# A hybrid encoder block on one core: the delta rule's stream moved to the front of the scan, and the order of the y blocks in the output projection

## The chip, the core and the metric

The kernel runs on one core of a Trainium2 chip. The time is device microseconds of one execution. The engines: PE (TensorE, with its weight load PEld), DVE (VectorE), ACT (ScalarE), POOL (GpSimd) and SP (SyncE, which issues most of the transfers). Each engine takes its instructions strictly in the order of its queue.

## What is computed

One encoder block on x of 512 tokens by 2048 features, in fp32. After a norm and one input projection, 16 heads of 128 go through two recurrences, 8 heads each, each scanned in both directions and summed; then a norm by head with a gate, one output projection, a residual sum, and a SwiGLU feed-forward.

```python
# group A, gated delta rule, per chunk of 64 (fwd and bwd summed)
w = u_c - einsum("bhrk,bhkv->bhrv", wk_c, S0)
o = einsum("bhrk,bhkv->bhrv", qd_c, S0) + einsum("bhrj,bhjv->bhrv", a_c, w)
S1 = gl_c * S0 + einsum("bhjk,bhjv->bhkv", kd_c, w)
# group B, HGRN2, per chunk of 32 (fwd and bwd summed)
A = sum(q_c * k_c * dec); o = (q_c * exp(Bc)) @ S0 + A @ v_c
S1 = exp(Bc[-1]) * S0 + (k_c * exp(Bc[-1] - Bc)).T @ v_c
# then: y = gated norm of both groups by head; x + y @ w_out; SwiGLU block
```

The recurrences of different heads don't depend on one another. The output projection sums over all heads of both groups.

## The kernel before

**Stages.** Projections of the input up to about 849 us of the span, then the scan, the output projection, gate and up, and down. The big products are split in high and low parts (oh, ol for the operands; whr, whs, wlr, wls for the weights) and done by seven products of half blocks.

**The scan** (`scan`, L836) runs two kinds of streams beside one another, each in pairs of heads 0, 2, 4, 6.

The delta rule is called gdn. `gdn_blocks` (L537) inverts the blocks of a pair: it loads tile L, sets P0 and P1 to zero (POOL, L549), loads into them, and goes through small matmuls L569/570, L578/579, L593/594 and L600/601 with transposes L586/587 on DVE. `gdn_pair` (L607) then does the recurrence of the pair: loads kq2 (L613, L614), vt, qd (L625); kt on DVE (L624); qd and L are multiplied on POOL (L626, L627). There are four steps. In a step: ks on PE (L645, not in the first step), rr on DVE (L649), matmul by P (L653), copy to w on ACT (L656), state on PE (L660) and S on DVE (L668 in the first step, L665 after), and the output oT on PE (L632). kq2, kt and qd have one buffer each; L has one for each of two pools, which the pairs take in turn. The blocks of the next pair run beside the recurrence of a pair.

HGRN2 is called hgrn (`hgrn_pair`, L678): loads hf, hq, hv (L686 to L688), four arrays X (ACT, DVE L694, POOL L695) and kc (POOL L697), then levels of 1, 2, 4, 8 and 16 and of 32 and 64: a copy kc on ACT (L719), matmuls (L722, L738), a predicated copy to C on DVE (L725), four updates of X on DVE (two of L748 and two of L750), and a product tot on POOL (L753) that the next level's updates need. At the end come transposes and their copies hkt, three steps with L781 and the state hS (L785, L788), and the output oT by L771 and L794. X of pairs 0 and 4 lies in one pool, X of pairs 2 and 6 in another, with one buffer each.

Each pair of either kind ends with `finish` (L437): squares, a sum by a matmul with ones (L445), ln and exp on ACT, two products on DVE (L448 and, with the gate gt loaded at L450, L451) and the store to d_y (L452).

**What sets the order.** The two kinds and the pairs are Python generators that yield a modelled time behind each part. `merge` (L815) takes the next part always from the stream whose modelled time is least; the first named wins a tie. A pair of numbers and streams like (40, a, b) is one stream that begins at 40 of modelled time and runs a, then b. A scheduler that simulates the engines' time lines then orders the instructions within what the code's order and the dependencies allow. Before, hgrn pairs 0 and 4 begin at 0, hgrn pairs 2 and 6 at 40, and gdn at 40, with hgrn's parts counted at 0.75 of their modelled time.

**The output projection** (`out_proj`, L870) first loads y back in blocks of two heads' pairs (tile yt, L892), in the order `Y_BLOCKS`: entry 0 is heads 0 to 3 of gdn, 2 its heads 4 to 7, 4 heads 0 to 3 of hgrn, 6 its heads 4 to 7. `operands` (L945) makes tsum (DVE, L941 to L943), oh (ACT, L956) and ol (DVE, L958) from each. `block_weights` (L962) loads the weights (raw, L972), sums them on DVE (L974 to L976), and splits them (L980 to L986). `step` issues the big matmuls (L1022) in the same order of blocks. The first tile yt lies, before and after, in memory that X of hgrn pairs 2 and 6 used, so its load waits until these are done.

Of the kernel before, what the change touches and what calls it, by code (L numbers as in the profile page):

```python
# [70 lines left out]
class Block:  # L71
# [769 lines left out]
    def scan(self):  # L841
        tc = self.tc
        with ExitStack() as st:
            pool = lambda name, **k: st.enter_context(tc.tile_pool(name=name, reuse_waits="tile", **{"bufs": 1, "side": "right", **k}))
            for n, b in (("psh", 2), ("pss", 2), ("poh", 1), ("pog", 1)):
                setattr(self, n, st.enter_context(tc.tile_pool(name=n, bufs=b, space=PSUM, reuse_waits="tile")))
            first, second, rest = pool("sca"), pool("scb"), pool("scc")
            self.sca = Pools(rest, hf=first, hq=first, C=first, X=second)
            self.sch, self.fin = pool("sch"), pool("fin")
            self.scb = pool("sc1"), pool("sc2", side="left")  # L850
            self.sc = pool("sc")
            self.gdn_ready = {}

            def gdn():
                yield from self.gdn_blocks(0)
                for i in range(0, H, 2):
                    yield from self.merge((0, self.gdn_pair(i)), *([(0, self.gdn_blocks(i + 2))] if i + 2 < H else []))

            def faster(i):
                for dt in self.hgrn_pair(i):  # L860
                    yield 0.75 * dt

            for _ in self.merge((0, faster(0), faster(4)), (40, faster(2), faster(6)), (40, gdn())):
                pass


    Y_BLOCKS = (0, 4, 6, 2)
    Y_SLOTS = (6, 7, 0, 1, 2, 3, 4, 5)

    def out_proj(self, late):  # L870
# [17 lines left out]
        yops = [None] * (KT // 2)  # L888
        for q, j in enumerate(self.Y_BLOCKS):
            for b in range(2):  # L890
# [3 lines left out]
        for ps in ((0, 1), *((p,) for p in range(2, KT // 2))):  # L894
            prods = self.block_products([(a["w_out"][0], 2 * p * P) for p in ps], 0, yops, order=self.Y_BLOCKS)
            for p, prod in zip(ps, prods):
# [292 lines left out]
```

## Time and profile before

| | us |
|---|---|
| median of 3 runs | 2677.78 (2677.45 to 2679.18) |
| the profiled execution | 2677.02 |
| its span | 2675.2 |
| PE busy | 2489.8 (93% of the span) |
| DVE busy | 2298.1 (86%) |
| ACT busy | 1497.4 (56%) |
| POOL busy | 519.9 (19%) |
| mean granted PE clock | 0.968 of full |

PE is the fullest engine over the whole span. The 40 slices of the page (66.9 us each) show where it isn't: in slices 13 to 17, about 803 to 1137 us, PE is 60 to 90% busy, and the granted clock is down to 0.8 there. That is the scan and the beginning of the output projection, and the views in the rows below are of that part. A busy share there is an average over places with different limits.

### The profile page before, as it was taken

To read this page: it belongs to the slowest core of one execution; us is meant where nothing else is said; L and a number is where in the kernel's file an instruction comes from. 1 tells how busy PE (TensorE), PEld (TensorE's weight loads), DVE (VectorE), ACT (ScalarE), POOL (GpSimd) and SP (SyncE) were. 2 spreads that over 40 slices of the span, in tenths; PEclk is the share of its full clock that TensorE was granted. 3 is DMA by queue.
4 is the path that set the end of the run, shared out by engine and by line. 5 is a ranking of instruction groups with operands and counts; after the bars stand their busy time and mean duration, and the time that the engine had idled before them with its cause. 6 is when DMAs were issued, how large, how long until landed. Compare 5 with 4: busy or idle time off the path is not lost.

```text
span 2675.2 us, 55501 instructions
## 1 busy us (share of the span) xinstructions
PE 2489.8 (93%) x22511; PEld 2437.7 (91%) x22511; DVE 2298.1 (86%) x3598; ACT 1497.4 (56%) x2057; POOL 519.9 (19%) x400
## 2 busy tenths in 40 slices
PE   7999999989997788799999999999999989998996
PEld 6999999889986667799899999999999989998996
DVE  7989989998976876877988989889889888888885
ACT  7787777666665433656644444444444455655664
POOL 1233224443333532222000000000000012222221
PEclk9999999999998888999999999999999999999998
DMA  8889999999897443799343344333333388887875
GB/s 228 191 200 210 212 204 223 232 220 239 200 233 201 108 122 113 220 243 251 118 135 127 123 123 126 122 116 121 125 114 123 121 250 196 213 190 178 195 157 142
DMA packets 401708, 465.71 MB, mean 174 GB/s; under 512 B 48449, under 2 KB 354043, under 8 KB 401451
## 3 DMA queue, kind: packets, MB, share of 16 engines
q1 hardware_dynamic: 310939, 311.67, 38.3%
q0 software_dynamic: 71936, 103.83, 24.2%
q10 hardware_dynamic: 18576, 46.67, 5.0%
q8 instruction: 176, 2.88, 0.4%
q14 instruction: 81, 0.66, 0.1%
HBM read 303.66 MB, written 54.62 MB: 134 GB/s over the span
## 4 chain that ended last, share of the span: by engine, by line
PE 67%; DMA 10%; DVE 9%; issue 7%; ACT 4%; POOL 1%; SPq 1%; ACTq 0%; DVEq 0%; POOLq 0%
PE big L1022 64%; DMA wlr<-raw 4%; DMA raw<-in_w_out 1%; DVE X L750 1%; DVE wls L986 1%; DVE X L748 1%; DMA acc<-d_rows 1%; DMA tt<-d_t 1%; DMA raw<-in_w_down 1%; ACT wlr L980 1%; ACT whs L985 0%; ACT whr L981 0%; DVE wsum L975 0%; DMA sl<-d_l 0%; DVE wsum L974 0%
## 5 line engine op out<-in xcount | busy, mean ns | idle before, releaser
L985 ACT CAST whs<-wsum 128x1024 fp32r<-128x1024 f32 (+1 forms) x448 | 461.8, 1033 | 470.2 <-PE big L1022 242.4
L986 DVE TENSOR_TENSOR wls<-wsum,whs 128x1024 fp32r<-128x1024 f32 (+1 forms) x448 | 563.2, 1258 | 151.4 <-ACT whs L985 146.7
L982 POOL DMA_DIRECT2D wlr<-raw x272 | 323.7, 1190 | 1889.1 <-DVE tsum L941 893.8
L1022 PE MATMUL big<-oh,whs 128*128 128x256 f32 x2368 | 661.8, 283 | 3.7 <-ACT whs L985 3.7
L1022 PE MATMUL big<-ol,whs 128*128 128x256 f32 x2368 | 661.4, 282 | 0.0
L1022 PE MATMUL big<-oh,wls 128*128 128x256 f32 x2368 | 646.4, 283 | 3.3 <-DVE wls L986 3.3
L1022 PE MATMUL big<-oh,wlr 128*128 128x256 f32 x1776 | 493.4, 282 | 23.0 <-DMA wlr<-raw 22.8
L1022 PE MATMUL big<-oh,whr 128*128 128x256 f32 x1776 | 499.4, 283 | 13.2 <-ACT oh L956 9.8
L1022 PE MATMUL big<-ol,whr 128*128 128x256 f32 x1776 | 496.7, 281 | 0.6 <-DVE ol L958 0.6
L1022 PEld LDWEIGHTS big<-oh,whs 128*128 128x128 f32 x2368 | 449.9, 190 | 5.0 <-ACT whs L985 5.0
L1022 PEld LDWEIGHTS big<-ol,whs 128*128 128x128 f32 x2368 | 450.4, 190 | 0.0
L1022 PEld LDWEIGHTS big<-oh,wls 128*128 128x128 f32 x2368 | 443.3, 191 | 4.4 <-DVE wls L986 3.9
L1022 PEld LDWEIGHTS big<-oh,wlr 128*128 128x128 f32 x1776 | 332.9, 189 | 26.8 <-DMA wlr<-raw 26.5
L1022 PEld LDWEIGHTS big<-oh,whr 128*128 128x128 f32 x1776 | 335.7, 189 | 17.5 <-ACT oh L956 12.6
L974 DVE TENSOR_TENSOR wsum<-raw 128x512 f32<-128x512 f32 (+1 forms) x448 | 314.5, 703 | 42.0 <-DMA raw<-in_w_out 20.2
L1022 PEld LDWEIGHTS big<-ol,whr 128*128 128x128 f32 x1776 | 335.2, 189 | 1.9 <-DVE ol L958 1.7
L1022 PE MATMUL big<-tp,whs 128*128 128x256 f32 x1728 | 322.8, 283 | 2.7 <-ACT whs L985 2.7
L981 ACT CAST whr<-raw 128x768 fp32r<-128x768 f32 (+1 forms) x272 | 221.6, 815 | 157.2 <-PE big L1022 155.9
L1022 PEld LDWEIGHTS big<-tp,whs 128*128 128x128 f32 x1728 | 270.0, 192 | 3.9 <-ACT whs L985 3.1
L1022 PE MATMUL big<-tp,wls 128*128 128x256 f32 x864 | 242.7, 286 | 24.4 <-DVE wls L986 24.4
L980 ACT ACTIVATE wlr<-raw 128x768 fp32r<-128x768 f32 (+1 forms) x272 | 224.4, 825 | 58.9 <-DMA raw<-in_w_out 23.6
L985 ACT CAST whr<-raw 128x768 fp32r<-128x768 f32 x176 | 146.8, 835 | 159.0 <-PE big L1022 156.8
(319 smaller groups left out, 4699.4 us busy)
## 6 DMA issues: line engine op xcount, KB each, us to landing
wlr<-raw POOLq DMA_DIRECT2D x256, 384.0 KB, 5.9
raw<-in_w_in SPq DMA_DIRECT2D x144, 512.0 KB, 4.9
raw<-in_w_gate SPq DMA_DIRECT2D x88, 512.0 KB, 3.6
raw<-in_w_up SPq DMA_DIRECT2D x88, 512.0 KB, 3.6
raw<-in_w_down SPq DMA_DIRECT2D x80, 512.0 KB, 4.6
raw<-in_w_out SPq DMA_DIRECT2D x32, 512.0 KB, 5.9
d_t<-yt ACTq DMA_DIRECT2D x22, 512.0 KB, 2.9
tt<-d_t ACTq DMA_DIRECT2D x22, 512.0 KB, 4.5
```

The costliest lines, as they stand in the source:

```text
L748: nc.vector.tensor_tensor(out=xv[:, 0:2, n, 0, :], in0=xv[:, 0:2, n, 0, :], in1=tv[:, :, n, 1:2].broadcast_to([P, 2, nb // 2, hs]), op=ALU ...
L750: nc.vector.tensor_tensor(out=xv[:, 2:4, n, 1, :], in0=xv[:, 2:4, n, 1, :], in1=tv[:, :, n, 0:1].broadcast_to([P, 2, nb // 2, hs]), op=ALU ...
L974: tt(out=sm[:, :, 0:2], in0=raw[:, :, 0:1].broadcast_to([P, n, 2, P]), in1=raw[:, :, 1:3], op=ALU.add)
L980: nc.scalar.mul(out=lo, in_=src_, mul=-1.0)
L981: nc.scalar.copy(out=hi, in_=src_)
L982: nc.gpsimd.dma_start(out=lo.rearrange("p j x n -> p j (x n)").bitcast(F32), in_=src_.rearrange("p j x n -> p j (x n)"), accum_op=ALU.add)
L985: nc.scalar.copy(out=hi, in_=src_)
L986: tt(out=lo, in0=src_, in1=hi.bitcast(F32), op=ALU.subtract)
L1022: mm = lambda a, b, s, e: nc.tensor.matmul(prod[i], lhsT=a, rhs=b, start=s, stop=e, skip_group_check=True)
```

## The change

The scan's `merge` gets its streams in another order: gdn is named first and begins at 0, with its parts counted at 0.8 of their modelled time; hgrn 0 and 4 begin at 0 as before, hgrn 2 and 6 at 40 as before. `paced` is the former `faster` with the factor as an argument. And the output projection takes the blocks of y in the order gdn 0 to 3, hgrn 0 to 3, gdn 4 to 7, hgrn 4 to 7, where hgrn 4 to 7 came ahead of gdn 4 to 7 before. No instruction of the computation is added or left out. Behind the change, the line numbers of the kernel after are larger by one.

```diff
-            def faster(i):
-                for dt in self.hgrn_pair(i):
-                    yield 0.75 * dt
-
-            for _ in self.merge((0, faster(0), faster(4)), (40, faster(2), faster(6)), (40, gdn())):
+            def paced(steps, x):
+                for dt in steps:
+                    yield x * dt
+
+            hgrn = lambda i: paced(self.hgrn_pair(i), 0.75)
+            for _ in self.merge((0, paced(gdn(), 0.8)), (0, hgrn(0), hgrn(4)), (40, hgrn(2), hgrn(6))):
                 pass
 
-    Y_BLOCKS = (0, 4, 6, 2)
+    Y_BLOCKS = (0, 4, 2, 6)
```

**DVE, gdn pair 2.** In the queue of DVE before, around the second and third rr of the pair (X_11312 belongs to hgrn 4, sh_11984 to the finish of another pair):

```order
L649 SCALAR_TENSOR_TENSOR rr_11933<-sc_11928,ngam_1220,vt_11626 128x128 x4
L748 TENSOR_TENSOR X_11312<-X_11312,tot16_11926 128x2x8x32
L750 TENSOR_TENSOR X_11312<-X_11312,tot16_11926 128x2x8x32
L748 TENSOR_TENSOR X_11312<-X_11312,tot16_11926 128x2x8x32
L750 TENSOR_TENSOR X_11312<-X_11312,tot16_11926 128x2x8x32
L448 SCALAR_TENSOR_TENSOR sh_11984<-oT_11616,cols_307,sh_11984 128x1024
L451 TENSOR_TENSOR sh_11984<-sh_11984,gt_11993 128x1024
L665 SCALAR_TENSOR_TENSOR S_11950<-S_11722,glast_1222,sc_11945 128x128 x4
L649 SCALAR_TENSOR_TENSOR rr_12002<-sc_11997,ngam_1220,vt_11626 128x128 x4
```

The same place of DVE after, from the pair's first S to the first S of pair 4 (kt_11703 and S_11795 are pair 4's, X_10971 is of hgrn 2):

```order
L668 COPY S_11136<-sc_11131 128x512
L586 STREAM_TRANSPOSE q64_11068<-P0_11070 32x32 x8
L587 STREAM_TRANSPOSE q64_11068<-P1_11079 32x32 x8
L649 SCALAR_TENSOR_TENSOR rr_11285<-sc_11280,ngam_1220,vt_11040 128x128 x4
L665 SCALAR_TENSOR_TENSOR S_11302<-S_11136,glast_1222,sc_11297 128x128 x4
L649 SCALAR_TENSOR_TENSOR rr_11391<-sc_11386,ngam_1220,vt_11040 128x128 x4
L665 SCALAR_TENSOR_TENSOR S_11408<-S_11302,glast_1222,sc_11403 128x128 x4
L649 SCALAR_TENSOR_TENSOR rr_11437<-sc_11432,ngam_1220,vt_11040 128x128 x4
L624 TENSOR_TENSOR kt_11703<-sc_11705,kdc_1221 128x1024
L624 TENSOR_TENSOR kt_11703<-sc_11714,kdc_1221 128x1024
L448 SCALAR_TENSOR_TENSOR sh_11516<-oT_11064,cols_307,sh_11516 128x1024
L451 TENSOR_TENSOR sh_11516<-sh_11516,gt_11525 128x1024
L668 COPY S_11795<-sc_11790 128x512
L748 TENSOR_TENSOR X_10971<-X_10971,tot8_11584 128x2x16x16
```

Before, updates of X stand between the rr of a pair; after, none stands between the three rr of pair 2, and the next update of X is queued behind the first S of pair 4.

**PE, the end of the scan.** Before, from the last L794 on (oT_12891 is the output of hgrn 6, the rows of L622, L653, L660, L632 and L645 are gdn 6's; the first big matmul of the output projection stands 16 rows below the first row here):

```order
L794 MATMUL oT_12891<-X_12107,hS_13005 128x128 x4
L622 MATMUL sc_12918<-ident_61,kq2_12911 128x128 x4
L622 MATMUL sc_12927<-ident_61,kq2_12911 128x128 x4
L653 MATMUL sc_12937<-vt_12912,P0_12394 128x128
L653 MATMUL sc_12937<-vt_12912,P1_12403 128x128
L653 MATMUL sc_12937<-vt_12912,P0_12394 128x128
L653 MATMUL sc_12937<-vt_12912,P1_12403 128x128
L445 MATMUL sc_13056<-sq_13053,ones_69 128x512
L445 MATMUL sc_13059<-sq_13053,ones_69 128x512
L660 MATMUL sc_12944<-w_12942,kt_12916 128x128 x4
```

PE after, from the last L794 of hgrn 6 on:

```order
L794 MATMUL oT_13045<-X_12504,hS_13066 128x128 x4
L794 MATMUL oT_13045<-X_12504,hS_13080 128x128 x4
L445 MATMUL sc_13096<-sq_13093,ones_69 128x512
L445 MATMUL sc_13099<-sq_13093,ones_69 128x512
L1023 MATMUL big_13274<-oh6_13164,whr_13284 128x256
L1023 MATMUL big_13277<-oh6_13164,whr_13284 128x256
L1023 MATMUL big_13275<-oh6_13164,whr_13284 128x256
```

Before, the whole recurrence of gdn 6 stands behind hgrn 6's last output; after, it stands ahead of it, and the output projection follows hgrn 6's finish.

**POOL, around gdn pair 2.** After, the two-input products that stand in one row on POOL beside the stretch of DVE above (L626 of gdn 2, L627 of gdn 4, L695 and L697 of hgrn 4):

```order
L753 TENSOR_TENSOR tot1_11956<-hf_11649 128x2x512
L626 TENSOR_TENSOR qd_11045<-qd_11045,kq2_11039 128x1024 x2
L753 TENSOR_TENSOR tot2_12113<-tot1_11956 128x2x256
L753 TENSOR_TENSOR tot64_12016<-tot32_11842 128x2x8
L695 TENSOR_TENSOR X_11655<-hq_11648,hf_11649 128x1024
L753 TENSOR_TENSOR tot4_12205<-tot2_12113 128x2x128
L697 TENSOR_TENSOR kc_11660<-X_11655 128x1024
L627 TENSOR_TENSOR L_11065<-L_11065,tri_78 128x1024 x2
```

The same products of gdn 2 and hgrn before stand apart from one another, with products tot between them:

```order
L753 TENSOR_TENSOR tot1_12231<-hf_12101 128x2x512
L626 TENSOR_TENSOR qd_11631<-qd_11631,kq2_11625 128x1024
L753 TENSOR_TENSOR tot2_12298<-tot1_12231 128x2x256
L626 TENSOR_TENSOR qd_11631<-qd_11631,kq2_11625 128x1024
L753 TENSOR_TENSOR tot4_12361<-tot2_12298 128x2x128
L753 TENSOR_TENSOR tot64_12173<-tot32_12073 128x2x8
L627 TENSOR_TENSOR L_11651<-L_11651,tri_78 128x1024 x2
L695 TENSOR_TENSOR X_12107<-hq_12100,hf_12101 128x1024
```

Between the two, the hgrn pair whose L695 stands beside gdn 2 is another: pair 6 before (X_12107), pair 4 after (X_11655).

## Rows read from the trace of the kernel before

**Rows 1.** Stretches: start:end, length, PE, PEld, DVE, ACT, POOL busy (instructions), clock, DMA, GB/s

```profile
849.00:1070.00 221.00, 166.24 (x3254) 143.29 (x3255) 164.35 (x315) 89.71 (x157) 86.53 (x67) 0.83 0.43 126
1070.00:1146.00 76.00, 60.90 (x445) 55.90 (x444) 63.26 (x111) 45.99 (x64) 15.48 (x11) 0.96 0.81 225
1146.00:1274.00 128.00, 124.82 (x1051) 124.13 (x1051) 102.94 (x160) 78.92 (x97) 27.69 (x23) 1.00 0.99 246
```

**Rows 2.** Chain of waits that ends last, 1040 to 1090: start, length, what

```profile
1070.47 0.52 SPq L892
...
1071.04 9.88 DMA yt<-d_y
...
1080.99 0.92 ACT oh L956 x2
```

**Rows 3.** Groups on DVE, 1070 to 1146: line, operation, count | busy, mean ns | idle before

```profile
L974 DVE TENSOR_TENSOR wsum<-raw 128x512 f32<-128x512 f32 x9 | 6.9, 766 | 4.5 <-DMA raw<-in_w_out 4.3
...
L448 DVE SCALAR_TENSOR_TENSOR sh<-oT,cols,sh 128x1024 f32<-128x1024 f32 x3 | 3.8, 1280 | 0.0
...
L451 DVE TENSOR_TENSOR sh<-sh,gt 128x1024 f32<-128x1024 f32 x3 | 3.7, 1220 | 0.0
L649 DVE SCALAR_TENSOR_TENSOR rr<-sc,ngam,vt 128x128 f32<-128x128 f32 x12 | 3.4, 345 | 0.0
...
L624 DVE TENSOR_TENSOR kt<-sc,kdc 128x1024 f32<-128x1024 f32 x2 | 2.4, 1220 | 1.9 <-PE sc L622 1.9
L665 DVE SCALAR_TENSOR_TENSOR S<-S,glast,sc 128x128 f32<-128x128 f32 x8 | 2.2, 344 | 0.2 <-PE sc L660 0.2
```

**Rows 4.** Time line of DVE: start, length, line, operation, [idle before <- what ended it]

```profile
1050.95 1.11 DVE L649 SCALAR_TENSOR_TENSOR rr<-sc,ngam,vt 128x128 f32<-128x128 f32 x4
...
1059.36 1.13 DVE L649 SCALAR_TENSOR_TENSOR rr<-sc,ngam,vt 128x128 f32<-128x128 f32 x4 [2.65 <-PE sc L645]
...
1080.56 0.68 DVE L668 COPY S<-sc 128x512 f32<-128x512 f32 x1
...
1084.30 1.12 DVE L649 SCALAR_TENSOR_TENSOR rr<-sc,ngam,vt 128x128 f32<-128x128 f32 x4
...
1109.22 1.12 DVE L649 SCALAR_TENSOR_TENSOR rr<-sc,ngam,vt 128x128 f32<-128x128 f32 x4
...
1136.52 0.69 DVE L941 TENSOR_TENSOR tsum<-yt 128x512 f32<-128x512 f32 x1 [3.60 <-DMA yt<-d_y]
...
1144.65 1.22 DVE L958 TENSOR_TENSOR ol<-tsum,oh 128x1024 fp32r<-128x1024 f32 x1
```

**Rows 5.** SP's issues of transfers (time line), and a transfer of the chain of waits

```profile
1000.33 0.36 SPq L613 DMA_DIRECT2D kq<-d_k  x1
...
1010.02 11.82 DMA L<-d_L
...
1126.21 0.36 SPq L452 DMA_DIRECT2D d_y<-sh  x1
```

**Rows 6.** Groups on DVE in the scan, 849 to 1070, shapes kept apart

```profile
L748 DVE TENSOR_TENSOR X<-X,tot 128x512 f32<-128x512 f32 x48 | 46.6, 972 | 26.9 <-PE sc L722 18.4 <-ACT hkt L766 3.0 <-PE sc L738 2.7
L750 DVE TENSOR_TENSOR X<-X,tot 128x512 f32<-128x512 f32 x48 | 45.5, 947 | 0.0
...
L750 DVE TENSOR_TENSOR X<-X,hf 128x512 f32<-128x512 f32 x8 | 5.5, 686 | 0.0
...
L587 DVE STREAM_TRANSPOSE q<-P 32x32 f32<-32x32 f32 x32 | 3.5, 169 | 0.9 <-ACT P L583 0.8
```

**Rows 7.** Time lines of DVE and POOL near 870

```profile
870.70 2.51 DVE L748 TENSOR_TENSOR X<-X,tot 128x512 f32<-128x512 f32 x1
873.13 2.82 DVE L750 TENSOR_TENSOR X<-X,tot 128x512 f32<-128x512 f32 x1
...
872.61 5.56 POOL L627 TENSOR_TENSOR L<-L,tri 128x1024 f32<-128x1024 f32 x2
```

**Rows 8.** Waits of PE in 849 to 1070: total us, times, longest

```profile
PE sc L569 <- DMA L<-d_L: 5.9, 1, 5.9
```

## The prediction

> **What bounds the kernel now.** I read the busy time by stage first [rows 1]. In 849 to 1070 us, where the scan runs with both streams, no engine is full: PE is busy 166.2 of 221 us, DVE 164.4. From 1146 to 1274 the output projection is bound by PE, 124.8 of 128 us at full clock, and nothing that the change does can shorten these 128 us. So the question is only when that stretch begins, and two marks set it. The chain of waits gives the first: the last matmul of hgrn pair 6 (L794) ends, and 1070.47 SP issues the load of the first block of y (yt), which lands 9.88 us later; its cast to an operand starts at 1080.99 [rows 2]. This load waits for hgrn 6 and not for the delta rule, since yt lies on memory that holds X of hgrn pairs 2 and 6. The second mark is the last operand of y, ol at 1144.65 for 1.22 us, so 1145.87 [rows 4]. Between the two lies what I call the ramp, 1145.87 - 1070.47 = 75.4 us. In it gdn pair 6, the last of the delta rule, runs beside the operands of y, and DVE, with 63.3 us of work in 76 [rows 1], is the fuller of the engines.
>
> So time = T (end of hgrn 6's L794) + ramp + a fixed rest. The change moves T later and shortens the ramp. The measure is the difference of two terms: X, by which T grows, and Y, by which the ramp shrinks.
>
> **Part 1: what moves.** By the order, gdn's instructions now stand in front of hgrn 6 on all engines, and hgrn 6's last L794 is followed at once by its own ones matmuls and the first matmul of the output projection. So all of gdn 6 that lies behind 1070 before is now ahead of T. Its DVE work there [rows 3]: L448 3.8 and L451 3.7, L649 3.4, L624 2.4, L665 2.2, and the copy L668 0.68 [rows 4], 16.2 us in all. One of the three finishes in these rows, 1.28 + 1.22 = 2.5, is hgrn 6's own and stays behind T. That leaves 13.7 us of DVE work that moves ahead. PE's share of it has room (166 of 221).
>
> **Part 2: does the scan stay as well filled?** If DVE idled as before, 1 - 164.35/221 = 25.6%, X would be 13.7 us or a little more. The order of DVE says that there is one stretch where it fills worse: in gdn pair 2, from its first S (L668) past three rr and two S to the S of pair 4, no instruction of hgrn stands on DVE or, but for one L794, on PE. In before four or five X updates stand between one rr and the next. X of hgrn 2 at level 8 is queued behind pair 4's L668. That stretch lasts as long as gdn's own chain:
> First S to the first rr: 1080.56 to 1084.30, 3.7 us. Two steps, each at least what one took while hgrn filled around it, 1050.95 to 1059.36 = 8.4, so 16.8 [rows 4]. Together 20.5 us to the third rr.
> Then pair 4 needs the single kq2 buffer, which pair 2 reads until this rr; on PE its first products stand behind L569 of the next blocks, which need tile L, whose buffer pair 2 also holds to its end. In before, from the issue of that kq2 load to L landed: 1000.33 to 1010.02 + 11.82 = 1021.84, 21.5 us [rows 5].
> From there to S the row from rr to S would be 4.65; I take 3.5 for the part behind rr, an estimate. Sum 20.5 + 21.5 + 3.5 = 45.5 us.
> DVE's work in it: L668 twice 1.4, rr three times 1.12 = 3.4, S twice 4 x 0.344 = 2.7, kt twice 1.22 = 2.4, a finish 2.5, and sixteen transposes, half of 3.5 [rows 3, 4, 6] = 1.7; together 14.1. Idle 45.5 - 14.1 = 31.4. At before's share it would be 0.256 x 45.5 = 11.6. So 19.8 us are new.
>
> **Part 3: what comes back.** X updates (L748, L750 on tot) take 0.972 and 0.947 us on average, against 0.686 for the same size where POOL is not beside them; 96 of them make 46.6 + 45.5 - 96 x 0.686 = 26.2 us lost in the scan [rows 6]. The loss stands where POOL multiplies two tiles: 870.70 and 873.13 took 2.51 and 2.82 while POOL did two L627 and, by the order, an L626 ahead of them, so 1.82 + 2.13 = 3.95 us over three POOL operations, 1.3 each [rows 7]. In the new order six such operations of POOL (L626 twice, L695, L697, L627 twice) come in the stretch where DVE is idle anyway. Relief: 6 x 1.3 = 7.9 us. Its ends are 0 (the collisions only move) and 6 x 2.13 = 12.8.
>
> X = 13.7 + 19.8 - 7.9 = 25.6 us, so T = 1096.
>
> **Part 4: the ramp.** DVE keeps 63.3 - 13.7 = 49.6 us there. It can't begin on y until the first load has landed, 1070.47 to 1080.99 = 10.5 us [rows 2], in which it has only sums of weights. In before gdn 6 filled this. So 60.1, and Y = 75.4 - 60.1 = 15.3 us. Ends: if weight sums fill all of the first wait, 49.6 and Y = 25.8; if the wait for raw of 4.3 [rows 3] comes on top, 64.4 and Y = 11.0.
>
> **Part 5: edits that I cost at nothing.** Y_BLOCKS: before, the block of gdn 4 to 7 is last and waits for the store of gdn 6 at 1126.21; at 1136.52 DVE had been idle 3.60 us for it [rows 4, 5]. In the new order that store is old, and the last block is that of hgrn 4 to 7, whose store follows T by the length of its finish, while three blocks are still to be done. Were this cover gone, it would cost the same 3.6. These 3.6 are not counted as a gain, since the DVE sum above has no idle time but that of the first wait. On SP the loads of gdn (kq2, P, qd, L) move ahead of hgrn 6's hq and hf; the buffers they need are free by then, and hgrn 6 waits for its X memory and not for them. The first three raw loads of w_out now stand behind hgrn 6's gt load on SP, which waits for the finish of hgrn 4: still ahead of T. The factor 0.75 of hgrn is as before; gdn's new factor acts on the order alone.
>
> **Sum.** X - Y = 25.6 - 15.3 = +10.3 us. On the profiled run, 2677.02, that gives 2687.3; the median of the three runs is 0.8 above that run, which is within the rounding of the terms. I predict 2687. A measurement of this kernel can tell about 0.2%, 5.4 us, so "same" is 2672.4 to 2683.1.
>
> **A rule weighed against the rows.** The collisions of [rows 7] fit what the Trainium skill says ("SBUF — State Buffer", "Who interferes with whom"): a DVE instruction with two inputs in SBUF contends with a GpSimd one that reads SBUF, and whoever comes second blocks wholly until the first is done. By that rule a POOL operation beside an idle DVE costs nothing, and the relief would be at the upper end, 12.8; the sum would then be +5.4 in place of +10.3. The 2.13 of the one row would speak for it, the mean of 1.3 against it: not every POOL operation meets an update.
>
> **Rivals.**
> Same: the stretch is shorter and the relief full. If the L load has landed early, the end of the stretch is gdn's finish, which in before came 1109.22 to 1126.21, 17.0 us behind the third rr [rows 4, 5]: 20.5 + 17.0 = 37.5, idle 23.4, less 9.6, so 13.8; X = 13.7 + 13.8 - 12.8 = 14.7, Y 15.3: -0.6, 2676.4. For it: PE waited for L only 5.9 us, and once, in the whole scan [rows 8]. Against it: that L goes into pair 2's buffer and cannot be early.
> Faster: the rest of the scan fills better by as much as the stretch fills worse, so that X is only 13.7; and weight sums fill the first wait, Y = 25.8. Then -12.1, 2664.9; with half of one of the two about 2670. For it: PE and DVE both have a quarter of the scan idle, and gdn's chain, now early, no longer trails behind. Against it: queues are in order, no hgrn instruction stands in the stretch, and no row names a place where the rest gains more than the 7.9 of part 3.
> Slower by much: the stretch is lengthened by the L load (PE's 5.9 of [rows 8] each time), no relief, and raw late. 51.4 long, idle 37.3 less 13.2 = 24.1; X = 37.8, Y = 11.0: +26.8, 2704. It decides from the point where L lands later than kq2.
> That gdn does not go ahead of hgrn 6 is excluded by the order.
>
> **How the numbers follow.** Forecast with its neighbours on the slower side (2683 to 2704) 0.48, of which a tenth beyond 2704; same 0.28; faster 0.24, of which half below 2667. The likeliest case's own range is 2680 to 2700. The range for 8 in 10 is 2666 to 2704. Faster by over 0.2% 0.24, within 0.2% 0.28, slower by over 0.2% 0.48.
>
> **What would show it.** After: the last L794 and the issue of yt near 1096 (X), the last ol near 1156 and the end of the output projection near 1284 (Y). DVE idle for some 31 us in one stretch of about 45 between gdn 2's first S and gdn 4's, with POOL busy in it; the mean of L748 on tot well under 0.972. If T is under 1085, part 2 is wrong; if the ramp is under 55 or over 65, part 4. If the rest behind the ramp is not 128 us, the frame of the whole is wrong.

## The result: slower by 1.1%, and the profile after

| | before | after |
|---|---|---|
| median, us | 2678.48 (2677.45 to 2685.65, 4 runs) | 2709.73 (2703.11 to 2720.29, 4 runs) |
| the profiled execution, us | 2677.02 | 2703.11 |
| its span, us | 2675.2 | 2701.3 |

The ratio is 1.0112 (95% interval 1.0089 to 1.0135), some 31 us. The forecast was 2687, with a range of 2666 to 2704: right in sign, in the place and in most of the terms, but a third of the size, and the time lies 6 us outside the range. The profiled execution is the fastest of the four of after, so marks of one trace are compared with marks of the other, not with the medians.

Both profiles can be cut at the same four places: the last combine of the projections (ACT's copy from big to t), the end of hgrn 6's last L794 and the issue of yt that follows it at once, the end of the last ol, and the combine of the third column of the output projection. The lines of after for the first three, from the time lines of ACT, SP and DVE (start, length, engine, line, operation):

```profile
833.82 0.35 ACT L1036 COPY t<-big 128x256 f32<-128x256 f32 x1
...
1100.87 0.88 SPq L893 DMA_DIRECT2D yt<-d_y  x2
...
1155.77 1.22 DVE L959 TENSOR_TENSOR ol<-tsum,oh 128x1024 fp32r<-128x1024 f32 x1
```

The line of before for the first mark:

```profile
841.35 0.35 ACT L1035 COPY t<-big 128x256 f32<-128x256 f32 x1
```

| stretch, us | before | after | difference |
|---|---|---|---|
| start to the projections' last combine | 841.4 | 833.8 | -7.5 |
| to the end of hgrn 6 (the scan) | 229.1 | 267.0 | +37.9 |
| to the last operand of y (the ramp) | 75.4 | 56.2 | -19.2 |
| to the combine of the third column | 24.9 | 33.9 | +9.0 |
| third column to the last combine of gate and up | 987.3 | 985.5 | -1.8 |
| from there to the last combine of down | 490.8 | 498.5 | +7.7 |

The first row and the last are chance. Up to the scan the order of all engines is the same in every kernel of this study, and yet that mark stands anywhere from 833.8 to 845.1 in the profiles. The down stage takes 488.1 to 498.5 us over them; the seven kernels that have one order of instructions in it (after, e1, e2, e6, e7, e8, e9) took 491.0 to 498.5. What the change did lies between: +37.9 - 19.2 + 9.0 = +27.7 us.

**The scan.** Busy times in the scan, cut at the marks, first before and then after (columns as in [rows 1]):

```profile
841.35:1070.45 229.10, 169.91 (x3458) 146.49 (x3457) 170.45 (x321) 93.32 (x164) 93.71 (x74) 0.84 0.44 129
```

```profile
833.82:1100.80 266.98, 191.59 (x3604) 164.77 (x3602) 179.08 (x349) 101.00 (x172) 103.56 (x76) 0.85 0.42 125
936.76:978.74 41.98, 28.74 (x352) 23.62 (x350) 14.85 (x43) 15.04 (x25) 16.35 (x9) 0.92 0.41 120
```

DVE has 8.6 us more work ahead of hgrn 6's end and 29 us more idle time: 58.6 of 229.1 before, 87.9 of 267.0 after. The second row of after is the stretch in gdn pair 2: 42.0 us long with 14.85 of DVE work, 27.1 idle. Here it is on DVE's time line, from the pair's first S to the first update of X behind pair 4's first S (in brackets the idle time before a row, and what ended it):

```profile
936.76 0.69 DVE L668 COPY S<-sc 128x512 f32<-128x512 f32 x1
938.95 0.84 DVE L586 STREAM_TRANSPOSE q<-P 32x32 f32<-32x32 f32 x8 [1.50 <-ACT P L582]
940.20 0.88 DVE L587 STREAM_TRANSPOSE q<-P 32x32 f32<-32x32 f32 x8 [0.40 <-ACT P L583]
942.42 1.13 DVE L649 SCALAR_TENSOR_TENSOR rr<-sc,ngam,vt 128x128 f32<-128x128 f32 x4 [1.35 <-PE sc L645]
945.97 1.12 DVE L665 SCALAR_TENSOR_TENSOR S<-S,glast,sc 128x128 f32<-128x128 f32 x4 [2.41 <-PE sc L660]
949.70 1.13 DVE L649 SCALAR_TENSOR_TENSOR rr<-sc,ngam,vt 128x128 f32<-128x128 f32 x4 [2.61 <-PE sc L645]
953.24 1.12 DVE L665 SCALAR_TENSOR_TENSOR S<-S,glast,sc 128x128 f32<-128x128 f32 x4 [2.42 <-PE sc L660]
955.92 1.13 DVE L649 SCALAR_TENSOR_TENSOR rr<-sc,ngam,vt 128x128 f32<-128x128 f32 x4 [1.56 <-PE sc L645]
963.85 2.36 DVE L624 TENSOR_TENSOR kt<-sc,kdc 128x1024 f32<-128x1024 f32 x2 [6.81 <-PE sc L622]
966.13 1.27 DVE L448 SCALAR_TENSOR_TENSOR sh<-oT,cols,sh 128x1024 f32<-128x1024 f32 x1
967.44 2.57 DVE L451 TENSOR_TENSOR sh<-sh,gt 128x1024 f32<-128x1024 f32 x1
978.05 0.69 DVE L668 COPY S<-sc 128x512 f32<-128x512 f32 x1 [8.04 <-PE sc L660]
979.76 0.69 DVE L748 TENSOR_TENSOR X<-X,tot 128x512 f32<-128x512 f32 x1 [1.01 <-PE sc L722]
```

Every idle time in it but the last is gdn waiting for itself. The two long ones stand ahead of pair 4. kt waited 6.81 us for its products on PE (L622, from 963.16), which stand there behind gdn 2's last outputs and the ones products of its finish (L445, from 961.26); the kq2 loads, issued at 955.94 and 956.35, took 3.9 to 4.8 us and had landed by then. Pair 4's first S waited 8.04 us, of which PE stood 6.7 for tile L. In the scan as a whole DVE's waits for gdn's own products grew, before first and then after (total, times, longest):

```profile
DVE rr L649 <- PE sc L645: 5.2, 4, 2.7
...
DVE S L665 <- PE sc L660: 1.5, 1, 1.5
```

```profile
DVE rr L649 <- PE sc L645: 18.3, 9, 2.6
...
DVE S L665 <- PE sc L660: 8.7, 6, 2.4
...
DVE kt L624 <- PE sc L622: 7.4, 2, 6.8
```

**The ramp.** The last operand is done 56.2 us behind hgrn 6's end, and the next combine 2.9 us behind that. But then the third column takes longer. PE's waits for this, from hgrn 6's end on, in after:

```profile
PE big L1023 <- ACT oh L957: 9.9, 3, 6.6
PE big L1023 <- DMA wlr<-raw: 7.8, 3, 5.3
PE big L1023 <- DVE ol L959: 1.2, 3, 0.4
```

In before the first two are 5.0 and 3.3 over the like stretch, and by 1146 PE had been taking matmuls of the output projection since 1085.62, beside gdn 6. In after it starts them at 1110.51 (first before, then after):

```profile
1085.62 0.39 PE L1022 MATMUL big<-oh,whr 128*128 128x256 f32 x1
```

```profile
1110.51 0.80 PE L1023 MATMUL big<-oh,whr 128*128 128x256 f32 x2 [6.63 <-ACT oh L957]
```

So when the last operand is done more of them are left. The same view for the big matmuls alone, from the last operand to the third column's combine (PE, PEld, DVE, ACT busy, clock, DMA, GB/s; first before, then after):

```profile
1145.87:1170.73 24.86, 22.56 (x190) 22.15 (x190) 4.75 (x8) 0.38 (x1) 1.00 0.95 234
```

```profile
1156.99:1190.87 33.88, 30.56 (x233) 30.36 (x234) 4.87 (x8) 0.37 (x1) 0.90 0.74 187
```

43 more matmuls at before's 22.56/190 = 0.119 us are 5.1 of the 9.0 us, an estimate; PE idles 1.0 us more, and the other 2.9 us go with a granted clock of 0.90 in place of 1.00.

### The profile page after: what moved, and what is told of

Read it like the earlier page. It is cut to its first block, busy times and chain, and to the rows that moved or that the text cites. A ratio compares the mean times of both kernels' runs of the same rounds, so it can differ in the third digit from the quotient of the medians.

```text
span 2701.3 us, 55526 instructions
## 1 busy us (share of the span) xinstructions
PE 2495.7 (92%) x22511; PEld 2441.5 (90%) x22511; DVE 2291.5 (85%) x3598; ACT 1498.1 (55%) x2057; POOL 526.6 (19%) x400
## 4 chain that ended last, share of the span: by engine, by line
PE 49%; DMA 4%; DVE 4%; issue 3%; ACT 2%; POOL 0%; ACTq 0%; POOLq 0%; DVEq 0%; SPq 0%
PE big L1023 46%; DMA wlr<-raw 2%; DMA raw<-in_w_down 1%; DVE ol L959 1%; DMA yt<-d_y 1%; DVE wls L987 0%; DMA tt<-d_t 0%; ACT oh L957 0%; PE oT L632 0%; DVE X L748 0%; DVE tsum L942 0%; PE oT L771 0%; DMA raw<-in_w_out 0%; DVE wsum L975 0%; DVE X L750 0%
## 5 line engine op out<-in xcount | busy, mean ns | idle before, releaser
L1023 PEld LDWEIGHTS big<-oh,wlr 128*128 128x128 f32 x1776 | 336.1, 191 | 35.4 <-DMA wlr<-raw 34.3
```

The lines of the kernel that those rows point to most:

```text
L1023: mm = lambda a, b, s, e: nc.tensor.matmul(prod[i], lhsT=a, rhs=b, start=s, stop=e, skip_group_check=True)
```

## The experiments

My theory after the result: the time is lost where gdn pair 2 stands alone, because DVE work that doesn't run there has to run later, at the rate of the rest of the scan. The first rival was that the loss comes from hgrn 6 ending last with nothing beside it; others were the order of the y blocks and the order of the down stage. The runs of before beside the experiments have medians of 2676.4 to 2680.7, and each ratio is to those beside it.

**The order of the y blocks alone, put back (e1).**

```diff
-    Y_BLOCKS = (0, 4, 2, 6)
+    Y_BLOCKS = (0, 4, 6, 2)
```

> The changed kernel with only the order of the y blocks put back (Y_BLOCKS 0, 4, 6, 2). The scan's order is that of the changed kernel. My theory: the loss sits in the scan (DVE idle in the stretch where gdn pair 2 stands alone, and the end of hgrn 6 later by 38 us), so this stays within 5 us of the changed kernel's 2709.7: 2705 to 2715, and the last L794 stays near 1101. Rival, the new y order starves PE in the third column of the output projection (the 6.7 us by which that column is longer in the profile of after): about 2703, and the third column back at 24 us.

2710.37 us (2701.97 to 2711.26), ratio to before 1.0125 (1.0105 to 1.0146): as the changed kernel. The scan took 271.1 us from the projections' last combine, and the third column was done 88.4 us behind hgrn 6's end (90.1 in after). The y order is not the cause.

**gdn named first in merge, nothing else (e2).** From the kernel before:

```diff
-            for _ in self.merge((0, faster(0), faster(4)), (40, faster(2), faster(6)), (40, gdn())):
+            for _ in self.merge((40, gdn()), (0, faster(0), faster(4)), (40, faster(2), faster(6))):
```

> The kernel before with its gdn stream named first in merge but still beginning at 40. The scan keeps the order of before but for one finish and two updates near its end; the down stage gets the same order of instructions as in the changed kernel. My theory: the 7.7 us by which the down stage was longer in the profile of after are chance between executions, so 2676 to 2681, and the down stage within 2 us of before. Rival, the order of the down stage costs them: 2684 to 2688, and the down stage 7 to 8 us longer than before.

2686.83 us, ratio 1.0042 (1.0025 to 1.0060), which is the rival's figure; but its mechanism is not what the profile shows. The down stage took 496.5 us, within what the same order gave elsewhere (491.0 to 498.5), and the scan 230.3, as before. 9 us are in the ramp: the third column was done 109.5 us behind hgrn 6's end, 100.3 in before; the last operand waited for gdn 6's store, which was issued at 1129.25, 62.3 us behind hgrn 6's end (55.8 in before, [rows 5]). So with a finish and two updates in another order near the end of the scan, and without a shift of the streams, this profile has a ramp that is 9 us longer; e5 has the same with another edit, so that the order is the cause is not shown. What in gdn 6 lost these 6.5 us I did not follow further.

**gdn at 0, but at its full modelled time (e3).** From the changed kernel:

```diff
-            for _ in self.merge((0, paced(gdn(), 0.8)), (0, hgrn(0), hgrn(4)), (40, hgrn(2), hgrn(6))):
+            for _ in self.merge((0, gdn()), (0, hgrn(0), hgrn(4)), (40, hgrn(2), hgrn(6))):
```

> The changed kernel with gdn's parts counted at their full modelled time instead of 0.8. gdn still begins at 0 and hgrn 6 still ends last, but the stretch in gdn pair 2 without any update of X on DVE is gone: two to eight updates stand between one rr and the next. My theory: the stretch of 42.0 us held 14.85 us of DVE work, which at the scan's share would have taken 20 us, so 22 us come back: last L794 near 1079, time 2688 (2682 to 2694). Rival, the loss is that hgrn 6 ends last with nothing beside it: the stretch is filled but the time stays above 2700.

2683.99 us (2676.26 to 2700.23, 9 runs), ratio 1.0029 (1.0010 to 1.0049). This is the run that decides. gdn still begins at 0, hgrn 6 still ends last, and of the 31 us 8 are left, each against before beside it. hgrn 6 is alone at the end for less time, though: 12.3 us from gdn's last output to its own last L794, against 36.6 in after (1064.16 to 1100.79). This first rival can be priced from after's own trace: the 36.6 us hold 24.0 of DVE work, which at before's share of 74.4% takes 32.3, so the lone end costs 4 us and not the 38 of the scan. In e9 below it lasts 70.2 us with 54.1 of work and costs nothing. The scan took 246.8 us, 20 less than in after:

```profile
839.52:1086.30 246.78, 192.44 (x3604) 165.62 (x3602) 181.43 (x348) 99.68 (x172) 100.75 (x76) 0.86 0.43 129
```

DVE idles 26.5% of it, near before's 25.6%. And the same steps of gdn 2 on DVE now have updates of X between them:

```profile
949.59 1.13 DVE L649 SCALAR_TENSOR_TENSOR rr<-sc,ngam,vt 128x128 f32<-128x128 f32 x4 [0.95 <-PE sc L645]
950.63 0.88 DVE L748 TENSOR_TENSOR X<-X,tot 128x512 f32<-128x512 f32 x1
951.43 2.85 DVE L750 TENSOR_TENSOR X<-X,tot 128x512 f32<-128x512 f32 x1
...
958.47 1.11 DVE L665 SCALAR_TENSOR_TENSOR S<-S,glast,sc 128x128 f32<-128x128 f32 x4
959.71 0.69 DVE L748 TENSOR_TENSOR X<-X,tot 128x512 f32<-128x512 f32 x1
960.32 0.69 DVE L750 TENSOR_TENSOR X<-X,tot 128x512 f32<-128x512 f32 x1
960.92 1.12 DVE L649 SCALAR_TENSOR_TENSOR rr<-sc,ngam,vt 128x128 f32<-128x128 f32 x4
...
971.81 1.13 DVE L649 SCALAR_TENSOR_TENSOR rr<-sc,ngam,vt 128x128 f32<-128x128 f32 x4 [0.60 <-PE sc L645]
```

From the second rr to the third it is 10.9 us here and 6.2 in after: gdn is slower with hgrn beside it, and the scan is faster for it.

**gdn alone twice (e9).** From the changed kernel:

```diff
-paced(gdn(), 0.8)
+paced(gdn(), 0.5)
```

> The changed kernel with gdn's parts counted at 0.5 of their modelled time instead of 0.8. In the order of DVE gdn now stands alone twice: in pair 2 and again in pair 4 (three rr each without an update of X between them). Theory: each such stretch costs what it lasts (42 us) less the 20 us that its DVE work would take at the scan's share, so a second 20 us or so: hgrn 6's last L794 some 290 us behind the last combine of the projections (269 in after), time 2724 to 2736. Rival, the loss of after is that hgrn 6 stands last and not the stretch: the same 269 us and 2705 to 2715.

2714.85 us (2711.88 to 2718.04), ratio 1.0147 (1.0118 to 1.0176); the scan 278.7 us, longer than the 267.0 to 271.3 of four profiles with after's scan (after, e1, e4, e8) but short of the expected 290. The time is a miss: it lies at the upper end of the rival's 2705 to 2715, and its ratio overlaps those of after and e1, so only the scan tells the two apart. The two stretches:

```profile
936.98:979.88 42.90, 27.36 (x343) 23.57 (x342) 13.49 (x43) 12.84 (x21) 16.34 (x9) 0.88 0.43 124
979.88:1013.70 33.82, 26.38 (x285) 21.46 (x283) 14.89 (x42) 9.87 (x16) 9.35 (x4) 1.00 0.19 63
```

In the second kt still waits 6.8 us for L622, but PE has no wait for tile L; it is 33.8 us long, not 42, with 14.9 of work: it costs 33.8 - 14.9/0.744 = 13.8 us and not 20. The sign in the scan is the theory's, the size was over-estimated.

**Two other starts (e10, e11).** From the changed kernel, gdn at 20 or at 40 with the factor 0.8:

```diff
-self.merge((0, paced(gdn(), 0.8)),
+self.merge((20, paced(gdn(), 0.8)),    # e11: 40
```

> gdn first in merge, at 0.8, beginning at 20 of modelled time instead of 0; y blocks in the new order, pools as in the changed kernel. No stretch with gdn alone; hgrn 6 and gdn 6 end together. Theory: 243 us from the projections to the last L794 as in e7_g20io, and a ramp 3 to 5 us longer than there for the later first load: 2683 to 2689. Rival, the pool of yt was no gain (e5 and e6 were slower with it than without): 2676 to 2682.

> gdn first in merge, at 0.8, beginning at 40 as in the kernel before; y blocks in the new order. Updates of X stand between all rr but two at the end of pairs; gdn 6 and hgrn 6 end together. Theory: DVE idles as in before (25.6%) and 13.7 us of DVE work lie ahead of hgrn 6's end, so the end is 14 to 18 us behind before's, and the ramp 11 us shorter: 2680 to 2688. Rival, side by side the two ends idle less than before's tail beside the ramp did: below 2674.

e10: 2685.28 us, ratio 1.0020 (1.0003 to 1.0038), scan 244.6, as expected. e11: 2691.53 us, ratio 1.0052 (1.0031 to 1.0072), slower than expected, though three rr of a pair never stand alone: its scan took 260.9. DVE had more work in it:

```profile
834.64:1095.55 260.91, 191.78 (x3600) 166.08 (x3598) 189.07 (x350) 97.75 (x169) 99.54 (x76) 0.84 0.41 124
...
L750 DVE TENSOR_TENSOR X<-X,tot 128x512 f32<-128x512 f32 x48 | 53.5, 1115 | 0.0
L748 DVE TENSOR_TENSOR X<-X,tot 128x512 f32<-128x512 f32 x48 | 44.9, 935 | 17.0 <-PE sc L722 11.0 <-issue 2.6 <-PE sc L738 1.2
```

The updates lose 53.5 + 44.9 - 96 x 0.686 = 32.5 us beside POOL, where before lost 26.2 [rows 6] and after 21.4. In all three traces the whole of it lies on updates that overlap an operation of POOL: 40 of the 96 in e11, 41 in before, 36 in after; the others took 0.686 us on average. So which updates meet POOL moves DVE's work by some 11 us between these orders. And one stretch does stand empty of updates in e11, around pair 2's last rr: from the S ahead of it at 982.04 to the end of pair 4's first S at 1008.49, 26.5 us with 9.9 of DVE work, kt waiting 7.4 us and S 7.8. By the rule for stretches below it costs 26.45 - 9.88/0.744 = 13.2 us.

**The memory of the first yt (e4, e5, e6, e7).** In e4 (changed kernel) and e5 (kernel before):

```diff
-        self.wst = pool("wst")
         self.io = pool("io")
+        self.wst = pool("wst")
```

e6 is e4 with e3's edit, e7 is e4 with e10's.

> The changed kernel with the pool of yt opened ahead of the pool of the weights, so that the first yt no longer lies on X of hgrn pairs 2 and 6; nothing else is changed by hand. My theory: the first operands of y (gdn heads 0 to 3, stored long before) can be made before hgrn 6 ends, so the wait of 10.5 us for the first load leaves the ramp: 2699 to 2705. Rival, DVE's sum bounds the ramp or the weights then wait for the same memory instead: within 3 us of 2709.7.

> The kernel before with only the pool of yt opened ahead of the pool of the weights, so that the first yt no longer lies on X of hgrn pairs 2 and 6. Theory: the ramp's first wait (10.5 us from hgrn 6's end to the first operand) can begin earlier, but in before gdn 6 fills DVE there, so little is gained: 2670 to 2677, the third column of the output projection at 95 to 100 us behind the last L794. Rival, the ramp is bound by that wait in before too: below 2668.

> The changed kernel with gdn at its full modelled time and the pool of yt ahead of the weights: e3_pace1 and e4_io together. Theory: the two gains lie in different stretches (the scan, the ramp) and add up. From e3's 2684.0, less the 5 to 7 us by which e4's third column stood nearer to the end of hgrn 6: 2677 to 2681. Its down stage has the order of the changed kernel; if that order costs 4 us as the four profiles so far suggest, 2681 to 2685. Rival, DVE bounds the ramp once the scan is filled: stays at 2684.

> gdn first in merge, at 0.8, but beginning at 20, and the pool of yt ahead of the weights. No place on DVE has three rr without an update of X between; hgrn 6 and gdn 6 end together (both finishes are the last two on DVE). Theory: as gdn 6 ends beside hgrn 6 and not behind it, X is the 18 us that 13.7 us of moved DVE work cost at 25.6% idle, and no stretch is lost; T about 18 us behind before's, ramp 17 shorter with the early yt: 2675 to 2682. Rival, the two ends side by side fill one another and the scan idles less: 2668 or below.

e4: 2704.77 us (2702.82 to 2712.31), 5 us less than the changed kernel but inside its spread, and its ratio of 1.0119 (1.0095 to 1.0143) is no smaller than the changed kernel's 1.0112, so no gain in time is shown; in its profile the third column was done 83.1 us behind hgrn 6's end, against 90.1 and 88.4, and PE no longer waited for the first operands there but 15.8 us for weights (wlr). e5: 2684.92, ratio 1.0018 (0.9999 to 1.0038), no gain and against my expectation the third column at 109.4 us behind hgrn 6's end instead of 100.3. e6: 2690.02, ratio 1.0029 (1.0012 to 1.0046): the two gains don't add up; PE waited 15.5 us for weights. e7: 2683.74, ratio 1.0016 (0.9994 to 1.0037), 2 us above the expected range; its scan took 242.9 us. To the third column it then needed 87.5 us, and e10, without the early yt, 87.4. So the first load's wait is there in the profile of e4, but the weights stand right behind it, and no time was gained by removing it.

**PE kept at work ahead of the output projection (e8).** In `finish`, for hgrn 6 only:

```diff
+        for i in range(6 if k == H + 6 else 0):
+            ps = pool.tile([P, T], F32, name="sc")
+            nc.tensor.matmul(ps, lhsT=self.ones, rhs=sq[:, i % 2], start=True, stop=True)
```

> The changed kernel with six extra products with ones on PE right behind hgrn 6's own two (results unused), some 6 us of work in the 6.6 us that PE idles ahead of the first matmul of the output projection; the computation is otherwise the same. In the profile of after the granted clock is 0.50 from 1112 to 1122 and 0.91 to 1132, so about 6 us of PE time are lost to the lower level. Theory: the clock there is a cost of the empty end of the scan; with PE at work the clock stays up and 3 to 6 us come back: 2703 to 2707. Rival, the operands of y bound the ramp and PE's clock does not matter: 2708 to 2712, or later by what the extra products push back.

2705.50 us (2701.57 to 2722.92): not to be told from the changed kernel by its time. The clock was at 1.00 while the products ran, and fell all the same behind them (start:end, length, PE busy, clock, DMA, GB/s):

```profile
1109.85:1119.70 9.85, 7.55 (x18) 1.00 0.85 207
1119.70:1130.00 10.30, 5.24 (x21) 0.68 1.01 285
1130.00:1140.00 10.00, 10.00 (x72) 0.81 0.78 221
```

The third column was done 88.2 us behind hgrn 6's end, as in e1 (88.4). Inconclusive on what the clock costs, since the operands still come one by one and the clock was not held.

**The y order in the kernel before (e12).**

```diff
-    Y_BLOCKS = (0, 4, 6, 2)
+    Y_BLOCKS = (0, 4, 2, 6)
```

> The kernel before with only the order of the y blocks changed to 0, 4, 2, 6; the scan's order is that of before. The block of gdn 4 to 7 now stands third, and its second half waits for the store of gdn 6 at the same time as before, with hgrn 4 to 7's block queued behind it on SP and DVE. Theory: the wait of 3.6 us moves forward and the last block, old by then, comes after it, so 2678 to 2686: about as before or up to 8 us slower. Rival, the order of the blocks is free: within 2 us of before.

2691.12 us, ratio 1.0051 (1.0029 to 1.0074), somewhat more than expected. The scan took 227.5 us and the third column 105.6 (100.3 in before), with 9.5 us of PE waiting for oh in place of 5.0. So the new order of the blocks is free in the changed kernel, where gdn ends early, and is slower where gdn 6 is last.

No version beats the kernel before: e3, e5, e7 and e10 come nearest, at 1.0016 to 1.0029 of it.

## Why the prediction was wrong in size, point by point

**What bounds the kernel, and the two marks.** Right: yt's load is issued 0.07 us behind the end of hgrn 6's last L794, at 1100.87. T was forecast at 1096; as the scan began 7.5 us earlier in this execution, T itself looks nearer than it was, and X is 37.9 us against 25.6.

**Part 1, what moves.** 13.7 us of DVE work were to move ahead of T. DVE's work up to T grew by 11.0 us in e3, 10.7 in e10 and 8.6 in after. With what POOL gave back added (1.5, 0.1 and 4.8) that is 12.5, 10.8 and 13.4. Right for after.

**Part 2, the stretch.** Right in place and nearly in size: 42.0 us long (45.5 forecast), 14.85 of DVE work in it (14.1), 27.1 idle (31.4). The scan of e3, without it, is 20 us shorter, so that it is the largest part of the loss.

**Part 3, what POOL gives back.** The updates lost 21.4 us in after against 26.2, so 4.8 came back, not 7.9. Nor were the six products in the stretch those that I had read off POOL's order: gdn 2's two L626 ran ahead of it, from 921.56 and 925.90, and two L626 of pair 4 ran in it. One of these met DVE there too: L451 at 967.44 took 2.57 us instead of 1.22, beside POOL's L626 from 966.58 to 968.92. That one row agrees with the rule that I had weighed (the Trainium skill, "SBUF — State Buffer", "Who interferes with whom": the later one is blocked until the earlier is done), since 968.92 + 1.22 = 970.14 is where it ends, 970.01; but the relief was not the upper end that I drew from the rule, as 36 updates still met POOL elsewhere. e11 shows that the same term can go the other way by 6.

**The step that failed: the sum X.** I added 13.7, 19.8 and -7.9 as they stood. But the frame was a scan in which DVE idles 25.6%, and there a microsecond of DVE work takes 1/0.744 us of time. 13.7 - 7.9 = 5.8 us of work are 7.8 us of time. And a stretch of 45.5 us replaces what its 14.1 us of work would have taken elsewhere, 14.1/0.744 = 19.0, and so costs 26.5 and not 19.8; what I had subtracted was the idle time that the stretch would have had by share, as if its length were given. With my own terms X is then 34.3, and the forecast 2677.0 + 34.3 - 15.3 = 2696. Measured is 37.9: the stretch costs 22.0, the work 8.6/0.744 = 11.6, and the 4.3 that are left are as much as the lone end of hgrn 6 costs by the same rule, a term that the forecast did not have. "X would be 13.7 us or a little more" is where it stood: it is 18.4, and e3, in which the stretch is gone, has a scan longer by 17.7.

The corrected sum was worked out after the result; this is how it holds over the kernels. The fourth column is DVE's work over 0.744, which fits before by its making; the last two are what is left and what the empty stretches explain, length less work over 0.744:

| kernel | scan, us | DVE work | work/0.744 | left | stretches |
|---|---|---|---|---|---|
| before | 229.1 | 170.45 | 229.1 | 0 | none |
| e7 | 242.9 | 180.88 | 243.1 | -0.2 | none |
| e10 | 244.6 | 181.12 | 243.4 | 1.2 | none |
| e3 | 246.8 | 181.43 | 243.9 | 2.9 | none |
| e11 | 260.9 | 189.07 | 254.1 | 6.8 | 13.2 |
| after | 267.0 | 179.08 | 240.7 | 26.3 | 22.0 |
| e9 | 278.7 | 177.73 | 238.9 | 39.8 | 24.8 + 13.8 |

Each row is one execution. Of the other profiles e6 leaves 0.4 us; e2, e5 and e12, with the scan of before or nearly so, -3.6 to -5.1; e1, e4 and e8, with the scan of after, 29.0 to 30.3, where their stretches explain 21.3 to 22.9. So the sum holds within some 9 us either way: enough to tell a stretch of 22 us, not the smaller terms.

**Part 4, the ramp.** To the last operand it was 56.2 us, forecast 60.1: the number is right, the wait in it only in part. DVE had 47.6 us of work there (49.6 forecast), but it idled 2.8 of the first 10.5 us and not all of them, since the sums of weights and the first tsum, from 1104.57, came in between; the rest of its 8.6 us of idle time fell later. And Y was taken at the wrong mark. "A fixed rest" behind the last operand is not fixed: PE starts the output projection 25 us later (1110.51 against 1085.62), has more of it left when the operands are done (233 matmuls to the third column, not 190), and the third column takes 33.9 us from there instead of 24.9. To that column Y is 100.3 - 90.1 = 10.2 and not 15.3. That is the second step that failed, by 5 us. In e4's profile the first load's wait is gone and 5 to 7 us with it (against e1 and after), and waits for weights stand in its place.

**Part 5, edits at nothing.** The y order: right for the changed kernel (e1). In e12, without gdn's early end as its cover, the time is 1.0051 of before's.

**The rivals.** "Slower by much" was the nearest, 2704, by another way: the stretch was not lengthened; one of ordinary length was only priced too low. The rule's variant and "same" both asked for a shorter stretch or full relief; neither came.

**What stays open.** With gdn 6 last, the time from hgrn 6's end to the third column was 100.3 us in before and 105.6 to 109.5 in e2, e5 and e12; why small shifts cost that much I have not settled. Nor is it settled how much of the third column is the lower clock; the 2.9 us above are what is left, not a measurement of it.

## What to carry to other kernels

Where two streams fill one another, price a move by the engine's work divided by its busy share in that stage, and a stretch in which one stream is alone by its length less that stage's time for the work in it; idle time alone is too small by the share. Here this held within some 9 us. Then look in the order of the queues for places where one chain stands alone: there it runs at its own latency (6.2 us a step here against 10.9 with the other beside it), and the quicker stream makes the whole slower. And when the work ahead of a bound stage is reshuffled, don't take the stage's rest as fixed: count what the bound engine has already done when the last operand comes.

## What the hardware showed that I had not expected

Executions with the same order differ by much: the mark at the end of the projections lay between 833.8 and 845.1 us over the profiles, and the down stage took 491.0 to 498.5 us over seven kernels with one order in it. Single profiles should be compared by stage.

PE's clock at the start of the output projection was at the lower level: in after the granted clock was 0.50, 1.2 GHz, from 1112 to 1122, behind the 6.63 us in which PE waited for the first operand (start:end, length, PE busy, clock, DMA, GB/s):

```profile
1112.00:1122.00 10.00, 7.00 (x28) 0.50 1.01 295
1122.00:1132.00 10.00, 10.00 (x79) 0.91 0.85 223
```

The collisions of DVE and POOL moved DVE's work in the scan by some 11 us between two orders of the same instructions (e11, 32.5 us lost; after, 21.4). Only updates that overlapped an operation of POOL were slow: the other 55 to 60 of 96 took 0.686 us on average in before, after and e11.
